# Half of the low parts of the MLP's second weight matrix: an accumulating DMA in place of a DVE subtraction

## The chip, the cores and the metric

One core of one Trainium2 chip. The metric is device microseconds of one execution of the whole program. The engines are named as the profile does: PE (TensorE, matmuls; PEld is its loading of weights), DVE (VectorE), ACT (ScalarE), POOL (GpSimd) and SP (SyncE, which here issues loads).

## The reference, cut to what matters

One decoder layer on 256 tokens of width 2048, all in float32: a normed input projection feeds sparse attention and retention, their gated sum is projected back, cross-attention and an MLP follow, and a final norm. The change touches the MLP's second product alone:

```python
def hybrid_layer(h, mem, ...):
    ...
    nm = rmsnorm(h, mlp_norm_w)
    h = h + jnp.square(jax.nn.relu(nm @ w_up)) @ w_down     # w_down: (8192, 2048), 64 MB
    return h

def reference(...):
    ...
    return rmsnorm(h, final_norm_w)
```

## The kernel before

Every weight passes through the core once, in chunks of 1 MB: 128 partitions by 2048 float32 values. A chunk's way is always the same. SP loads it from DRAM into a `raw` tile (three buffers). Then `chunk` cuts it into two halves of 1024 columns, and `split` makes two tiles of each half: ACT copies it to `hi`, rounded to the format that PE multiplies in one pass (float32r), and DVE subtracts, `lo = raw - hi`. `hi` and `lo` have four buffers each (`NHI`), so two chunks. The activations are split in the same way into a high and a low part. PE computes high times high, low times high and high times low, so three matmuls stand where one float32 product would be.

In `w_down` the activations are the stationary side (`xgroup`). For each row tile of 128 weights rows and each of the two token tiles, PE does `hi` with the activations' high part, `hi` with their low part, and `lo` with their high part, in that order, each over 512 columns: 12 matmuls per half, 24 per chunk. The product is done in two passes `f` over 4096 hidden channels, each after its own `w_up` stage; a pass has four column blocks `j` of 8 chunks. This makes 64 chunks. The first pass's `w_down` runs from about 1402 to 1559 us of the span, the second's from about 1765 to 1938 us.

In the last block (f = 1, j = 3) the last two chunks go through another branch of `xgroup` (`last`): both are loaded and split first, and then their matmuls run token tile by token tile. At the end of the first block of the second pass, `down_evac` takes one of the three `raw` buffers for the final norm's weights and keeps it to the end.

The work is written in the order of the main stream. A scheduler places each engine's instructions at build time, gives out the buffers and adds the waits: a buffer is given to a new tile when all readers of the old one are done, so the load of a new chunk waits for the last reader of an old `raw`, and the copy to a new `hi` for the last matmul with the old one. `pin` holds an order only in the program's first stage; here it does nothing.

POOL does a few small operations and DMAs in earlier stages. In the MLP it has nothing before the final norm's power.

Of the kernel before, what the change touches and what calls it, by code (L numbers as in the profile page):

```python
# [11 lines left out]
AF = mybir.ActivationFunctionType  # L12
ALU = mybir.AluOpType
# [4 lines left out]
P = 128  # L18
T = 256
D = 2048  # L20
EPS = 1e-6
# [44 lines left out]
class Kern:  # L66
# [15 lines left out]
        self.hung = 0  # L82
        self.ordered = False

    # ---- tiles
    def nm(self, s):
        self.n += 1
        return f"{s}_{self.n}"
# [22 lines left out]
    def pot(self, name):  # L111
        return self.po.tile([P, 512], F32, name=self.nm(name), tag="po")

    # ---- order: a step of the main stream is one tick; work hung on a later tick goes between steps
    def after(self, n, fn):
        self.hung += 1
        self.due.append((self.ticks + n, self.hung, fn))
# [11 lines left out]
        while self.due:  # L129
            self.tick()  # L130

    # streams in turns, each with its number of steps a turn
    def run(self, *gens):
        gens = [list(g) + [0.0] if isinstance(g, tuple) else [g, 1, 0.0] for g in gens]
        while gens:
            for item in list(gens):
                item[2] += item[1]
                while item[2] >= 1:
                    item[2] -= 1
                    try:  # L140
                        next(item[0])
                    except StopIteration:
                        gens.remove(item)
                        break
                    self.tick()
# [2 lines left out]
        for g in gens:  # L148
            yield from g

    # ---- arithmetic
    # while the pipeline fills, each engine keeps the order of the program
    def pin(self, ins):
        if self.ordered:
            self.tc.keep_in_program_order(ins)
# [1 line left out]
    def mul(self, out, l, r, start, stop):  # L157
        self.pin(self.nc.tensor.matmul(out, l, r, start=start, stop=stop, skip_group_check=True))  # L158

    # hi + lo == src, both exact in the tensor engine's one-pass format  # L160
    def split(self, hi, lo, src):
        self.pin(self.nc.scalar.activation(hi, src, AF.Copy))  # L162
        self.pin(self.nc.vector.tensor_tensor(lo, src, hi.bitcast(F32), op=ALU.subtract))  # L163

    # the same for src * scale, with a scale per partition
    def split_scaled(self, hi, lo, src, scale):
        self.pin(self.nc.scalar.activation(hi, src, AF.Copy, scale=scale))
        self.pin(self.nc.vector.scalar_tensor_tensor(lo, src, scale, hi.bitcast(F32), op0=ALU.mult, op1=ALU.subtract))

    # (v * s + EPS) ^ -0.5  # L170
    def rsqrt(self, out, v, s):
        self.nc.vector.tensor_scalar(out, v, s, EPS, op0=ALU.mult, op1=ALU.add)
        self.nc.gpsimd.tensor_tensor(out, out, self.mhalf.to_broadcast(out.shape), op=ALU.pow)
# [1 line left out]
    def bcast(self, R):  # L175
        return R[:, None, :].to_broadcast([P, 4, T])

    # tanh(y / 2) in place: sigmoid(y) = (1 + tanh(y / 2)) / 2
    def half_tanh(self, y):
        self.nc.scalar.activation(y, y, AF.Tanh, scale=0.5)  # L180

    # ---- the stream of weights
    def raw(self):
        return self.st.tile([P, 2048], F32, name=self.nm("raw"), tag="raw", bufs=3)

    # weights of kt row tiles, n columns; lists of hi and lo per row tile
    def chunk(self, src, kt, n, first=None):
        raw = self.raw()[:, :kt * n].rearrange("p (k n) -> p k n", k=kt)
        src = src.rearrange("(k p) n -> p k n", p=P)
        parts = 2 if first else 1  # L190
        for j in range(parts):
            if j:
                self.second()
            s = slice(j * kt // parts, (j + 1) * kt // parts)
            self.pin(self.nc.sync.dma_start(raw[:, s, :], src[:, s, :]))
        hs, ls = [], []
        m = 1024 // n
        for k in range(0, kt, m):
            h = self.st.tile([P, m, n], F32R, name=self.nm("hi"), tag="hi")
            l = self.st.tile([P, m, n], F32R, name=self.nm("lo"), tag="lo")  # L200
            self.split(h, l, raw[:, k:k + m, :])
            if first and k == 0:
                first()
            hs += [h[:, j, :] for j in range(m)]
            ls += [l[:, j, :] for j in range(m)]
        return hs, ls

    # out[col, t]: weights stationary
    def wgroup(self, w, c0, xh, xl, evac, rows=D):
        nkt = rows // P  # L210
        ps = self.mmt("w")
# [12 lines left out]
                evac(ps.rearrange("p (b t) -> p b t", b=4))  # L224
            yield

    # out[t, col]: activations stationary
    def xgroup(self, w, c0, xh, xl, evac, r0=0, rows=D, n=512, last=False, first=None):
        nkt = rows // P
        ps = [self.mmt("x")]  # L230
        ps = [self.mmt("x")[:, :n], ps[0][:, :n]] if last else [ps[0][:, 0:n], ps[0][:, 512:512 + n]]

        def part(kt, i, h, l):
            o = ps[i]
            s = slice(i * P, (i + 1) * P)
            a, c = xh[kt // 4][:, kt % 4, s], xl[kt // 4][:, kt % 4, s]
            self.mul(o, a, h, kt == 0, False)
            self.mul(o, c, h, False, False)
            self.mul(o, a, l, False, kt == nkt - 1)

        ck = 2048 // n
        end = nkt - 2 * ck if last else nkt
        for kt in range(end):
            k = kt % ck
            if k == 0:
                h, l = self.chunk(w[r0 + kt * P:r0 + (kt + ck) * P, c0:c0 + n], ck, n, first if kt == 0 else None)
            for i in range(2):
                part(kt, i, h[k], l[k])
            if kt == nkt - 1:
                for i in range(2):  # L250
                    evac(i, ps[i])
            yield
        if last:
            hs, ls = [], []
            for kt in range(end, nkt, ck):
                h, l = self.chunk(w[r0 + kt * P:r0 + (kt + ck) * P, c0:c0 + n], ck, n)
                hs += h
                ls += l
            for i in range(2):
                for kt in range(end, nkt):  # L260
                    part(kt, i, hs[kt - end], ls[kt - end])
                evac(i, ps[i])
                yield

    # four column tiles of src's two token tiles, transposed and split with the gain w
    def load_part(self, name, src, w, hs, ls, c, halves=False):
        x = self.big(name + "x", F32, (2, 512))

# [50 lines left out]

        return turn, split, spill, squares  # L320

    # 1 / rms per token, as a column and along each row
    def load_rms(self, s8, rs, R):
        nc = self.nc
        nc.vector.tensor_reduce(rs, s8, axis=AX.X, op=ALU.add)
# [59 lines left out]
    def retention(self):  # L385
        nc, a, rs = self.nc, self.a, self.rs
# [107 lines left out]

        self.ordered = True
        s8 = self.keep("xs8", [2, 4])
        # the tensor engine at its full clock by the time that the weights are there
        warm = self.pst("warm")

        def spin(n):  # L500
# [4 lines left out]
        turn, split, spill, squares = part(0)  # L505
# [8 lines left out]
        group = self.X(OFF["q_r"], rotary(qrT), first=rest)  # L514
        for c in range(4):
# [3 lines left out]
            if c < 3:  # L519
                turn, split, spill, squares = part(c + 1)  # L520
# [25 lines left out]
        self.flush()  # L546
        self.orh, self.orl = orh, orl

    # tanh of half the gate, tokens on the partitions
    def gate(self, dst):  # L550
        def evac(i, ps):
            if i == 0:
                dst.append(self.big("gate", F32, (2, 512)))
            self.nc.scalar.activation(dst[-1][:, i, :], ps, AF.Tanh, scale=self.hrs[:, i:i + 1])
        return evac
# [3 lines left out]
        self.nc.vector.tensor_tensor(o, ps, self.bcast(self.R), op=ALU.mult)  # L559
        self.kvc.append(o)  # L560

    # the overlapping windows of one of k, v with their position codes: [d, l, (g, c)], hi next to lo
    def blocks(self, which):
        nc = self.nc
        kT = self.kvc[which]
# [62 lines left out]
    def keys(self):  # L628
        nc, a, rs, R = self.nc, self.a, self.rs, self.R
        V, A, G, PE = nc.vector, nc.scalar, nc.gpsimd, nc.tensor  # L630
        self.mask = self.keep("mask", [800])
        self.tc.keep_in_program_order(nc.sync.dma_start(self.mask, a["c_mask"]))
        # columns of a group's keys: sel tile 1 | sel tile 0 | compressed | win tile 0 | win tile 1
        kcat = self.kcat = [self.big(f"kcat{g}", F32R, (2, 528)) for g in range(4)]
        self.vh, self.vl = {}, {}
        self.qh, self.ql = [], []
# [218 lines left out]
                          *[self.X(OFF["gate_a"] + 512 * j, self.gate(ga)) for j in range(4)]))  # L855
        self.flush()

    # h += f * ps; the split of h * w; the sum of squares
    def residual(self, dst, base, w, hs, ls, f, acc=None):
        nc = self.nc  # L860
        V, A = nc.vector, nc.scalar
# [22 lines left out]
    def merge(self):  # L884
        nc, a = self.nc, self.a
# [15 lines left out]
                        self.after(4 + 3 * n, lambda n=n: turn(j, n))  # L901
            return evac

        # the merged branches with channels on the partitions
        def turn(j, n):
            pt = self.pst("mT")
            for b in range(2):
# [117 lines left out]
    def mlp(self):  # L1025
        nc, a = self.nc, self.a
# [1 line left out]
        hres = [None] * 4  # L1028
        s8, r2 = self.keep("hs8", [2, 4]), self.keep("r2", [2])

        # the residual with tokens on the partitions, and its mean square
        def back(j, i):
            if i == 0:
                hres[j] = self.big("hres", F32, (2, 512))
# [24 lines left out]
        f8, ft = self.keep("fs", [2, 4]), self.keep("ft", [2])  # L1059
        fw, outs = [], []  # L1060

        # hidden = relu(u)^2 with u not yet divided by the rms: 1 / (mean square) at the end
        def down_evac(f, j):
            def evac(i, ps):
                o = hres[j][:, i, :]
# [29 lines left out]
        for f in range(2):  # L1095
            hh, hl = [], []
            self.run(self.seq(*[self.wgroup(a["w_up"][0], f * 4096 + 512 * j, self.h2h, self.h2l, up_evac(hh, hl))
                                for j in range(8)]))
            self.run(self.seq(*[self.xgroup(a["w_down"][0], 512 * j, hh, hl, down_evac(f, j), r0=f * 4096, rows=4096,
                                            last=(f == 1 and j == 3)) for j in range(4)]))  # L1100


def body(tc, a, out):
# [25 lines left out]
```

## Time and profile before

| | |
|---|---|
| Time, median of 2 runs | 1953.76 us (1953.6 to 1953.93) |
| Profiled execution, span from first to last instruction | 1951.9 us |
| Runs above that span | 1.9 us |
| PE / DVE / ACT / POOL busy, share of the span | 99% / 59% / 48% / 4% |
| Granted TensorE clock, mean | 0.999 |

The profiled execution has no time of its own beside its span; the 1.9 us are the difference to the median of the runs. A busy PE says that matmuls were in flight, not that they ran at the array's peak: a matmul's record is 0.40 us long here, and the next one starts before it ends. So the time of a stage is read from the starts.

### The profile page before, as it was taken

The page shows a single profiled execution, that of the slowest core. Times are in us where ns is not written, and L with a number is a line of the kernel's source. Part 1 is how long each engine was busy: PE and PEld are TensorE (multiplying, and loading weights), DVE is VectorE, ACT ScalarE, POOL GpSimd, SP SyncE. Part 2 cuts the span into 40 slices and gives each one's busy share as a digit, 9 for nine tenths or more (in the row PEclk, how much of TensorE's full clock was granted, in tenths as well). Part 3 has the DMA queues.
Part 4 walks back from the last instruction along what each step waited for, and adds up shares of the span by engine and source line. Part 5 has one row for each costly group of instructions (what it writes and reads, how often), then busy time and mean ns, then how long its engine had stood idle before and what let it go on. Part 6 is the DMA issues. An engine that isn't in the chain of part 4 may idle for free.

```text
span 1951.9 us, 28137 instructions
## 1 busy us (share of the span) xinstructions
PE 1933.5 (99%) x11606; PEld 1714.9 (88%) x11606; DVE 1145.7 (59%) x1327; ACT 937.3 (48%) x1214; POOL 85.3 (4%) x101
## 2 busy tenths in 40 slices
PE   8999999999999999999999999999999999999998
PEld 6888889888899999888889999999988899998886
DVE  6554577555756666886556756555544445554454
ACT  6444444454555555766445545544433344444442
POOL 1100021000000000321000000000000000000000
PEclk9999999999999999999999999999999999999999
DMA  7555544677876775434566654565655555655554
GB/s 269 210 174 192 186 172 175 229 249 245 274 248 244 248 254 176 137 112 140 184 208 232 208 173 154 172 191 177 193 184 184 193 189 179 189 178 194 188 179 151
DMA packets 190017, 382.29 MB, mean 196 GB/s; under 512 B 10576, under 2 KB 18768, under 8 KB 189760
## 3 DMA queue, kind: packets, MB, share of 16 engines
q1 hardware_dynamic: 185872, 375.01, 57.2%
q10 hardware_dynamic: 3216, 3.15, 0.5%
q0 software_dynamic: 800, 2.33, 0.4%
q8 instruction: 91, 1.49, 0.3%
q14 instruction: 38, 0.31, 0.0%
HBM read 374.17 MB, written 6.29 MB: 195 GB/s over the span
## 4 chain that ended last, share of the span: by engine, by line
PE 97%; DVE 1%; ACT 0%; issue 0%; DMA 0%; POOLq 0%; POOL 0%; DVEq 0%
PE x L158 52%; PE w L158 36%; PE acc L158 3%; PE o L158 1%; PE s L158 1%; PE ro L158 1%; PE pT L816 1%; DMA anw<-in_attn_norm_w_dram 0%; DVE lo L163 0%; PE tr L287 0%; PE rs L158 0%; ACT hi L162 0%; DVE bl L163 0%; PE xo L158 0%; PE g L158 0%
## 5 line engine op out<-in xcount | busy, mean ns | idle before, releaser
L163 DVE TENSOR_TENSOR lo<-raw,hi 128x1024 fp32r<-128x1024 f32 x688 | 848.6, 1240 | 702.8 <-ACT hi L162 688.1
L162 ACT ACTIVATE hi<-raw 128x1024 fp32r<-128x1024 f32 x688 | 724.1, 1059 | 913.2 <-PE x L158 526.0
L158 PE MATMUL w<-nh,hi 128*128 128x256 f32 x1088 | 308.2, 283 | 0.0
L158 PE MATMUL w<-nh,lo 128*128 128x256 f32 x1088 | 307.5, 283 | 0.0
L158 PE MATMUL w<-nl,hi 128*128 128x256 f32 x1088 | 306.9, 282 | 0.0
L158 PE MATMUL x<-hi,xh 128*128 128x512 f32 x704 | 282.5, 401 | 2.2 <-ACT hi L162 2.2
L158 PE MATMUL x<-hi,xl 128*128 128x512 f32 x704 | 278.0, 395 | 0.0
L158 PE MATMUL x<-lo,xh 128*128 128x512 f32 x704 | 277.2, 394 | 0.0
L158 PEld LDWEIGHTS w<-nl,hi 128*128 128x128 f32 x1088 | 207.1, 190 | 0.0
L158 PEld LDWEIGHTS w<-nh,hi 128*128 128x128 f32 x1088 | 207.1, 190 | 0.0
L158 PEld LDWEIGHTS w<-nh,lo 128*128 128x128 f32 x1088 | 206.8, 190 | 0.0
L158 PE MATMUL x<-hi,hl 128*128 128x512 f32 x512 | 202.7, 396 | 0.0
L158 PE MATMUL x<-hi,hh 128*128 128x512 f32 x512 | 202.3, 395 | 0.0
L158 PE MATMUL x<-lo,hh 128*128 128x512 f32 x512 | 201.0, 393 | 0.0
L158 PEld LDWEIGHTS x<-lo,xh 128*128 128x128 f32 x704 | 133.1, 189 | 30.9 <-DVE lo L163 0.8
L158 PEld LDWEIGHTS x<-hi,xh 128*128 128x128 f32 x704 | 132.8, 189 | 30.1 <-ACT hi L162 2.6
L158 PEld LDWEIGHTS x<-hi,xl 128*128 128x128 f32 x704 | 132.8, 189 | 26.5
L158 PE MATMUL w<-xh,hi 128*128 128x256 f32 x512 | 145.3, 284 | 0.0
L158 PE MATMUL w<-xh,lo 128*128 128x256 f32 x512 | 144.2, 282 | 0.0
L158 PE MATMUL w<-xl,hi 128*128 128x256 f32 x512 | 144.1, 281 | 0.0
L158 PEld LDWEIGHTS x<-lo,hh 128*128 128x128 f32 x512 | 96.6, 189 | 22.7
L158 PEld LDWEIGHTS x<-hi,hh 128*128 128x128 f32 x512 | 96.2, 188 | 23.1
(257 smaller groups left out, 2572.9 us busy)
## 6 DMA issues: line engine op xcount, KB each, us to landing
raw<-in_w_in_dram SPq DMA_DIRECT2D x119, 1024.0 KB, 4.9
raw<-in_w_up_dram SPq DMA_DIRECT2D x64, 1024.0 KB, 5.3
raw<-in_w_down_dram SPq DMA_DIRECT2D x64, 1024.0 KB, 5.1
raw<-in_cmp_w_k_dram SPq DMA_DIRECT2D x16, 1024.0 KB, 4.9
raw<-in_w_b_dram SPq DMA_DIRECT2D x16, 1024.0 KB, 5.2
raw<-in_cmp_w_v_dram SPq DMA_DIRECT2D x16, 1024.0 KB, 5.0
raw<-in_w_a_dram SPq DMA_DIRECT2D x16, 1024.0 KB, 5.1
raw<-in_w_out_dram SPq DMA_DIRECT2D x16, 1024.0 KB, 5.1
```

What stands on the lines that cost most here:

```text
L158: self.pin(self.nc.tensor.matmul(out, l, r, start=start, stop=stop, skip_group_check=True))
L162: self.pin(self.nc.scalar.activation(hi, src, AF.Copy))
L163: self.pin(self.nc.vector.tensor_tensor(lo, src, hi.bitcast(F32), op=ALU.subtract))
L816: PE.transpose(pt[:, r * P:(r + 1) * P], sms[r // 2][:, r % 2, c:c + P], self.ident)
```

## The change

`split_by_dma` takes the place of `split` for the second half of a chunk (`k` is 2) in the main loop of `w_down`; the first half keeps the subtraction. ACT writes `-round(raw)` into `lo`, GpSimd issues a DMA that adds `raw` onto `lo` in SBUF, and ACT copies `raw` to `hi`. `lo` is then `raw - round(raw)`, as before. The chunks of the `last` branch don't pass `adds` and stay as they were. The other lines of the diff take out comments.

```diff
+    def split_by_dma(self, hi, lo, src):
+        self.nc.scalar.activation(lo, src, AF.Copy, scale=-1.0)
+        self.nc.gpsimd.dma_start(lo, src, accum_op=ALU.add)
+        self.nc.scalar.activation(hi, src, AF.Copy)
...
-    def chunk(self, src, kt, n, first=None):
+    def chunk(self, src, kt, n, first=None, adds=False):
...
-            self.split(h, l, raw[:, k:k + m, :])
+            if adds and k:
+                self.split_by_dma(h, l, raw[:, k:k + m, :])
+            else:
+                self.split(h, l, raw[:, k:k + m, :])
...
-    def xgroup(self, w, c0, xh, xl, evac, r0=0, rows=D, n=512, last=False, first=None):
+    def xgroup(self, w, c0, xh, xl, evac, r0=0, rows=D, n=512, last=False, first=None, adds=False):
...
-                h, l = self.chunk(w[r0 + kt * P:r0 + (kt + ck) * P, c0:c0 + n], ck, n, first if kt == 0 else None)
+                h, l = self.chunk(w[r0 + kt * P:r0 + (kt + ck) * P, c0:c0 + n], ck, n, first if kt == 0 else None, adds)
...
-                                            last=(f == 1 and j == 3)) for j in range(4)]))
+                                            last=(f == 1 and j == 3), adds=True) for j in range(4)]))
```

## Rows read from the trace of the kernel before

**Rows 1.** The page: busy time by engine, and the chain by engine.
```profile
PE 1933.5 (99%) x11606; PEld 1714.9 (88%) x11606; DVE 1145.7 (59%) x1327; ACT 937.3 (48%) x1214; POOL 85.3 (4%) x101
...
PE 97%; DVE 1%; ACT 0%; issue 0%; DMA 0%; POOLq 0%; POOL 0%; DVEq 0%
```

**Rows 2.** Windows: busy us of PE, PEld, DVE, ACT, POOL, clock, DMA share, GB/s.
```profile
1402.50:1559.50 157.00, 157.00 (x678) 127.16 (x678) 74.80 (x64) 61.95 (x59) 0.00 (x0) 1.00 0.57 190
...
1810.00:1938.00 128.00, 128.00 (x552) 103.61 (x551) 62.50 (x62) 51.06 (x57) 0.00 (x0) 1.00 0.53 174
1938.00:1951.90 13.90, 5.46 (x24) 4.09 (x22) 5.67 (x12) 2.89 (x6) 1.10 (x2) 0.83 0.41 151
...
1934.50:1937.50 3.00, 3.00 (x15) 2.43 (x14) 0.00 (x0) 0.00 (x0) 0.00 (x0) 1.00 0.02 5
```

**Rows 3.** Timeline: matmul starts, and one half's copy and subtraction (start, length).
```profile
1403.41 0.40 PE L158 MATMUL x<-hi,hh 128*128 128x512 f32 x1
...
1406.44 0.40 PE L158 MATMUL x<-hi,hl 128*128 128x512 f32 x1
...
1419.44 1.06 ACT L162 ACTIVATE hi<-raw 128x1024 fp32r<-128x1024 f32 x1 [1.74 <-PE x L158]
...
1420.53 1.23 DVE L163 TENSOR_TENSOR lo<-raw,hi 128x1024 fp32r<-128x1024 f32 x1 [1.57 <-ACT hi L162]
...
1934.46 0.40 PE L158 MATMUL x<-hi,hl 128*128 128x512 f32 x1
...
1937.47 0.40 PE L158 MATMUL x<-lo,hh 128*128 128x512 f32 x1
```

**Rows 4.** Waits of POOL from 1390 to 1940 us: total us, times, longest.
```profile
POOL ft L1084 <- DVE ft L1083: 812.5, 1, 812.5
```

**Rows 5.** Lines from 1402.5 to 1559.5 us: busy us, mean ns, idle before.
```profile
L163 DVE TENSOR_TENSOR lo<-raw,hi 128x1024 fp32r<-128x1024 f32 x56 | 68.6, 1224 | 79.2 <-ACT hi L162 79.2
L162 ACT ACTIVATE hi<-raw 128x1024 fp32r<-128x1024 f32 x57 | 60.5, 1061 | 96.6 <-PE x L158 89.6 <-DVE lo L163 5.2 <-PE w L158 1.8
```

**Rows 6.** DMA of the first `w_down` stage: packets, MB, held share; us to landing.
```profile
q1 hardware_dynamic: 14962, 29.73, 56.7%
...
raw<-in_w_down_dram SPq DMA_DIRECT2D x28, 1024.0 KB, 5.1
```

**Rows 7.** Line 717, POOL's spill of `gate`: issue ns, us to landing.
```profile
L717 POOL DMA_DIRECT2D msp<-gate x4: 531/531/630, 482.9 to 562.6; - x4
...
DMA to landing us min/median/max: 3.2/3.3/3.5
```

**Rows 8.** DMA of 482 to 486 us and of 508 to 512 us.
```profile
q0 software_dynamic: 144, 0.52, 39.2%
...
raw<-in_w_b_dram SPq DMA_DIRECT2D x1, 1024.0 KB, 7.7
...
raw<-in_w_b_dram SPq DMA_DIRECT2D x1, 1024.0 KB, 5.3
```

**Rows 9.** SP's loads from 1775 us on (timelines), and waits from 1810 to 1935.
```profile
1789.35 0.34 SPq L1071 DMA_DIRECT2D raw<-in_final_norm_w_dram  x1
1794.90 128.77 SPq L195 DMA_DIRECT2D raw<-in_w_down_dram  x24
...
1822.85 0.37 SPq L195 DMA_DIRECT2D raw<-in_w_down_dram  x1
...
1839.55 0.37 SPq L195 DMA_DIRECT2D raw<-in_w_down_dram  x1
...
ACT hi L162 <- DMA raw<-in_w_down_dram: 7.8, 3, 2.8
...
SPq L195 <- DVE lo L163: 105.1, 21, 7.0
```

**Rows 10.** Windows of half a microsecond while one load runs (last: DMA share, GB/s).
```profile
1824.00:1824.50 0.50, 0.50 (x3) 0.38 (x2) 0.10 (x1) 0.37 (x1) 0.00 (x0) 1.00 0.80 82
...
1826.00:1826.50 0.50, 0.50 (x4) 0.41 (x3) 0.00 (x0) 0.40 (x1) 0.00 (x0) 1.00 1.04 406
```

## The prediction

> **What bounds the kernel now.** I read the page's busy line and its chain first: TensorE (PE) is busy for 99% of the span and makes up 97% of the chain that ended last [rows 1]. Then the stage of the change alone. The second multiplication of the MLP (`w_down`) runs twice, in the windows of [rows 2]: PE busy without a gap, DVE about 48%, ACT about 40%, the sixteen DMA engines 57% and 53%. Then the order inside the stage. A chunk is 512 rows of weights, split in two halves of 1024 columns, and each half feeds 12 matmuls that start 0.232 us apart [rows 3]. So a half lasts 2.79 us and a chunk 5.57 us, which is also the spacing of the loads, (1839.55 - 1822.85) / 3 [rows 9]. Last, the waits: ACT waits for PE to free a buffer, DVE waits for ACT, PE for nobody [rows 2, 5]. PE sets the pace; DVE, ACT and the loads follow it with time to spare.
>
> How much time: `hi` and `lo` have four buffers each, a buffer is free when PE has ended the half four back, and the new content is needed three halves later, 8.36 us. The copy to `hi` takes 1.06 us and the subtraction 1.23 us [rows 3, 5], so a half is ready about 6 us early.
>
> **The change, part by part.** The program has 64 chunks of `w_down`; the last two go through the `last` branch, which doesn't pass `adds`. So 62 odd halves change, one per chunk.
>
> *Removed:* 62 subtractions of 1.224 us [rows 5], 76 us of DVE. PE did not wait for DVE, so this gives 0. Could the matmuls run faster beside a quieter DVE? From 1934.5 to 1937.5 DVE and ACT are idle and the DMA engines nearly so [rows 2], and there 13 starts take (1937.47 - 1934.46) us, 0.232 us each; with all of them at work 13 take (1406.44 - 1403.41) us, 0.233 us each [rows 3]. So nothing is gained, and the bound below is 0.
>
> *Added on ACT:* 62 copies with scale -1, as long as the copy to `hi`, 1.06 us [rows 5]. ACT then does 3.2 us in a chunk of 5.57 us: hidden. The copy to `hi` of that half, now behind the negated copy in ACT's queue, is ready at about 2.2 us of its 8.36 us. If this cover were gone, each chunk would pay at most 1.06 us.
>
> *Added on GpSimd (POOL):* 62 DMA issues, 0.53 to 0.63 us each as in the spill of `gate` [rows 7]. POOL has nothing else to do from the last norm to the end, 812 us [rows 4], so nothing is queued behind a waiting issue: 0.
>
> *The wait that is added.* PE's third matmul of an odd half needs `lo`, and all later matmuls stand behind it. The negated copy ends 1.1 us after the buffer is free, so the DMA may take 8.36 + 0.46 - 1.1 = 7.7 us from issue to landing. No row shows a transfer from SBUF to SBUF or one that adds. The nearest are four POOL transfers of the same 512 KB from SBUF to DRAM: 3.2 to 3.5 us to landing [rows 7], in which the 16 engines were held for 39.2% of 4 us, 1.57 us [rows 8]. An addition reads two operands, `raw` and `lo`, and writes one. Lower bound: the second read costs nothing, 1.57 us held, 3.3 us to landing. Middle: the second read costs another pass, 3.14 us held, 4.9 us to landing. Upper: read, read and write follow one another, 4.7 us held, 6.5 us to landing. I take the middle, since it counts the bytes that must be read, and keep both ends. Even the upper end is under 7.7 us while the transfer is alone, so what decides is that it isn't alone.
>
> The weight loads hold the engines for 56.7% of the stage [rows 6], 0.567 x 5.57 = 3.16 us a chunk. Beside the first spill a 1 MB load took 7.7 us to land, beside the second 5.3 us, against 5.1 us in this stage [rows 6, 8]: the two queues can cost each other time, so I add up their held times. The Trainium skill says why ("DMA: Bandwidth & Descriptors", section "Issuing engines are not separate DMA queues"): DMAs from any issuing engine run on the same 16 DMA engines and interleave. By that rule the sum is the one below; by separate queues the change would cost nothing before the two-buffer stretch below. The 7.7 us row agrees, without proving it.
>
> Adding: 3.16 + 3.14 = 6.30 us of DMA engines in a chunk that PE does in 5.57 us. The DMA engines would then set the pace: 0.73 us x 62 = 45 us. With the lower end, 4.73 us, they don't; with the upper end, 7.87 us, it is 2.30 x 62 = 143 us.
>
> *The raw buffers.* The transfer also holds `raw` until it has landed, and the next load into that buffer, on SP's queue, waits for it (as it does for DVE now [rows 9]); behind it in SP's queue stand only later loads. For 40 chunks there are three raw buffers: the loop of load 5.1, copy 1.06, negated copy 1.06, transfer 4.9 and about 0.2 of wake-ups is 12.3 us of the 16.7 us that three chunks give. From the load of the final norm's weights at 1789 us on, one of the three is taken, and 24 loads go through two [rows 9]. There the loop has 11.14 us: a transfer above 3.7 us makes it the bound. It is already the one place where ACT waits for a load (7.8 us, three times) [rows 9]. With 4.9 us alone it asks for 6.2 us a chunk, under the 6.30 us above; if loads and additions fully stretch each other, 5.1 + 1.6 and 4.9 + 1.6, it is 7.7 us, and 22 chunks would pay 32 us more than counted. Against that stands that a load holds the engines while it hardly moves anything: in a half microsecond near its start 82 GB/s at a share of 0.80, later 406 GB/s [rows 10]. Packets of the other queue might move there. These two have opposite signs and similar size; I take neither.
>
> **Sum.** Removed 0, ACT 0, POOL 0, DMA engines +45 us on the profiled execution's 1951.9 us; the runs lie 1.9 us above the span, for work around it that the change doesn't touch. 1953.8 + 45 = 1999 us.
>
> **The rivals.**
>
> *Hidden.* The second read runs beside the write: 4.73 us held of 5.57. Only the two-buffer stretch could feel it: 3.3 us alone is under 3.7 us, stretched by up to 1.5 us it costs half of that less 0.4 over 22 chunks, at most 12 us. 1954 to 1966 us. For it: DMA share 57% and a short spill. Against it: two operands of 512 KB have to be read.
>
> *Bytes, not held time.* At the full rate of about 400 GB/s [rows 10] a load needs 2.6 us and two reads 2.6 us: 5.2 us, under 5.57, if the slow start of each transfer is filled by the other queue. Then only the two-buffer stretch pays: (12.3 - 11.14) / 2 = 0.58 us x 22 = 13 us, up to 30 us with some stretching: 1967 to 1985 us. The Trainium skill speaks for this one ("Collectives: The Full Stack", section "The bandwidth ceiling: the fold count and why AG ≠ RS ≠ AR"): an adding transfer is slower because it reads two sources, and the addition costs nothing. No row here shows it.
>
> *The addition is slower than its reads.* If a row's write waits for both of its reads, 4.7 us are held and PE runs at the DMA engines' 7.87 us a chunk in all 62: 2097 us, and more if the engines sit idle between the rows of one transfer. It decides from about 2.4 us held per addition, where 3.16 and the addition exceed 5.57. For it: the operation is one that no row shows, on every engine at once. Against it: nothing in the trace.
>
> *Faster.* It would need PE to run closer than 0.232 us, or a wait on DVE that PE doesn't have [rows 2].
>
> **How the numbers follow.** A measurement of this kernel can tell about 2%, 39 us, from no change. Forecast, 1985 to 2040 us: 0.34, of which 0.04 lies below 1993 us. Hidden: 0.17. Bytes: 0.22. Slower addition, 2040 us and above: 0.25. Faster: 0.02. So faster by over 2%: 0.02; within 2%: 0.17 + 0.22 + 0.04 = 0.43; slower: 0.30 + 0.25 = 0.55. The range goes from the hidden case, 1955 us, to the upper bound of the addition, 2100 us; beyond lie about half of the slowest case, 0.12, and some 0.06 below. The forecast's own range is 1985 to 2040 us.
>
> **What the changed profile would show.** DVE's `lo<-raw,hi` down by 62, ACT's copies up by 62, POOL with 62 issues. The software queue with 62 transfers of 512 KB, at some 28% (one pass), 50% (two) or more of the stage. The matmul with `lo` in the chain waiting for a POOL DMA, PE idle by 0.7 us a chunk, chunks 6.3 us apart, the DMA share near 1. If the bytes rival is right, three-buffer chunks stay at 5.57 us and the later ones spread. If the addition is slow, its landing takes over 7.7 us and the spacing is the same in both stretches. What would make the forecast wrong most of all is the held time of one addition, for which the nearest row is a plain transfer; then ACT's order, if the negated copy were put behind later copies; and the granted clock, which is 1.00 while PE is never idle and 0.83 in the last window, where it is [rows 2]: waits inside the stage might cost more than their length.

## The result, and the profile after

| | |
|---|---|
| Time, median of 2 runs | 2058.43 us (2055.69 to 2061.18) |
| Before | 1953.76 us |
| Ratio | 1.0536, 95% interval 1.0518 to 1.0553 |
| Profiled execution, span | 2053.9 us, before 1951.9 us |
| Granted TensorE clock, mean | 0.984, before 0.999 |

The change costs 105 us, 5.4%. The forecast was 45 us, so the direction was right and the size less than half. The page first, its busy line, its chain by engine and by line:

```profile
PE 1969.1 (96%) x11606; PEld 1729.7 (84%) x11606; DVE 1070.8 (52%) x1265; ACT 992.7 (48%) x1276; POOL 138.7 (7%) x163
...
PE 79%; DMA 15%; issue 3%; ACT 2%; DVE 1%; POOL 0%; POOLq 0%; SPq 0%; ACTq 0%; DVEq 0%
PE x L158 36%; PE w L158 35%; DMA lo<-raw 11%; DMA raw<-in_w_down_dram 3%; PE acc L158 3%; PE o L158 1%; ACT lo L167 1%; PE s L158 1%; ACT hi L169 1%; PE ro L158 1%; PE pT L825 0%; DVE lo L163 0%; DMA anw<-in_attn_norm_w_dram 0%; PE tr L296 0%; DMA rep<-in_c_rep_dram 0%
```

Against [rows 1]: DVE lost 75 us, ACT gained 55, POOL 53, and PE's share of the chain fell from 97% to 79%. What took its place is the adding DMA (`lo<-raw`, 11%) and the loads (3%), which were not in the chain before. PE's own busy time grew by 36 us for the same matmuls.

Next, where it happened. POOL issues one addition per chunk, so the spacing of its issues is the spacing of the chunks. The timeline of POOL, the first and last issue of the first pass (32 issues), and of a part of the second pass with one raw buffer gone (19 issues):

```profile
1399.62 0.92 POOL L168 DMA_DIRECT2D lo<-raw  x1 [271.83 <-ACT lo L167]
...
1595.14 0.86 POOL L168 DMA_DIRECT2D lo<-raw  x1 [6.54 <-ACT lo L167]
...
1863.55 0.86 POOL L168 DMA_DIRECT2D lo<-raw  x1 [5.17 <-ACT lo L167]
...
2023.80 0.86 POOL L168 DMA_DIRECT2D lo<-raw  x1 [8.01 <-ACT lo L167]
```

With three raw buffers a chunk takes (1595.14 - 1399.62) / 31 = 6.31 us, with two (2023.80 - 1863.55) / 18 = 8.90 us; before it was 5.57 us throughout. So 40 chunks lose 0.73 us each, 29 us, and 22 chunks lose 3.3 us each, 73 us: 102 us, the difference of the two spans. Most of the loss lies in the smaller part.

The two stretches have different bounds. The windows, PE's busy time first, the last three columns the granted clock, the DMA engines' share and GB/s:

```profile
1402.50:1590.00 187.50, 171.80 (x716) 135.05 (x714) 42.92 (x39) 93.42 (x92) 25.77 (x30) 0.98 0.92 246
...
1840.00:2040.00 200.00, 154.52 (x553) 116.36 (x552) 37.56 (x41) 70.04 (x80) 18.94 (x22) 0.88 0.68 174
```

And the DMA queues from 1402.5 to 1595.5 and from 1862 to 2024 us, q1 with the loads and q0 with the additions: packets, MB, share of the engines' time.

```profile
q1 hardware_dynamic: 15910, 31.60, 48.1%
q0 software_dynamic: 4387, 15.94, 44.3%
...
q1 hardware_dynamic: 9504, 18.88, 39.4%
q0 software_dynamic: 2593, 9.44, 29.4%
```

With three buffers the engines are held 92% of the time (before: 57% [rows 2, 6]), near a bound. With two they are held 68%: here they have time, and the chunks are still slower. What is late there is read from the chain between 1907 and 1925 us, one turn of one raw buffer (start, length, what):

```profile
1907.22 6.23 DMA raw<-in_w_down_dram
...
1914.52 1.04 ACT hi L169
1915.56 0.96 ACT lo L167
1916.52 0.28 issue
1916.80 8.13 DMA lo<-raw
...
1925.06 6.15 DMA raw<-in_w_down_dram
```

The load lands, ACT copies the first half to `hi` (0.96 us, from 1913.56), the second half to `hi` (1.04), negates (0.96), POOL starts 0.28 us later, the addition lands after 8.13 us, and only then does SP load into the buffer again: 1925.06 - 1907.22 = 17.84 us for two chunks, with PE nowhere in it. The waits from 1862 to 2024 us say the same, in total us, times and longest; the last is SP's:

```profile
ACT hi L162 <- DMA raw<-in_w_down_dram: 92.7, 17, 6.8
PEld x L158 <- DMA lo<-raw: 48.3, 19, 4.3
...
SPq L201 <- DMA lo<-raw: 159.4, 19, 9.0
```

One thing was not as the diff is written. ACT's timeline shows the copy to `hi` (line 169) ahead of the negated copy (line 167), in all 62 chunks; the scheduler had turned them round:

```profile
1408.63 1.06 ACT L169 ACTIVATE hi<-raw 128x1024 fp32r<-128x1024 f32 x1 [0.74 <-PE x L158]
1409.60 1.04 ACT L167 ACTIVATE lo<-raw 128x1024 fp32r<-128x1024 f32 x1
```

### The profile page after: what moved, and what is told of

Its sections match the earlier page's. It is cut to its first block, busy times and chain, and to the rows that moved or that the text cites. A ratio compares the mean times of both kernels' runs of the same rounds, so it can differ in the third digit from the quotient of the medians.

```text
span 2053.9 us, 28340 instructions
## 1 busy us (share of the span) xinstructions
PE 1969.1 (96%) x11606; PEld 1729.7 (84%) x11606; DVE 1070.8 (52%) x1265; ACT 992.7 (48%) x1276; POOL 138.7 (7%) x163
## 4 chain that ended last, share of the span: by engine, by line
PE 79%; DMA 15%; issue 3%; ACT 2%; DVE 1%; POOL 0%; POOLq 0%; SPq 0%; ACTq 0%; DVEq 0%
PE x L158 36%; PE w L158 35%; DMA lo<-raw 11%; DMA raw<-in_w_down_dram 3%; PE acc L158 3%; PE o L158 1%; ACT lo L167 1%; PE s L158 1%; ACT hi L169 1%; PE ro L158 1%; PE pT L825 0%; DVE lo L163 0%; DMA anw<-in_attn_norm_w_dram 0%; PE tr L296 0%; DMA rep<-in_c_rep_dram 0%
## 5 line engine op out<-in xcount | busy, mean ns | idle before, releaser
L163 DVE TENSOR_TENSOR lo<-raw,hi 128x1024 fp32r<-128x1024 f32 x626 | 773.1, 1242 | 871.3 <-ACT hi L162 848.8
L162 ACT ACTIVATE hi<-raw 128x1024 fp32r<-128x1024 f32 x626 | 658.0, 1058 | 886.1 <-PE x L158 358.6
L158 PE MATMUL x<-lo,hh 128*128 128x512 f32 x512 | 215.7, 423 | 65.5 <-DMA lo<-raw 65.4
L158 PE MATMUL x<-hi,hh 128*128 128x512 f32 x512 | 211.9, 414 | 0.5 <-ACT hi L162 0.4
L158 PE MATMUL x<-hi,hl 128*128 128x512 f32 x512 | 210.9, 412 | 0.0
L158 PEld LDWEIGHTS x<-lo,hh 128*128 128x128 f32 x512 | 102.1, 200 | 105.6 <-DMA lo<-raw 82.4
L158 PEld LDWEIGHTS x<-hi,hh 128*128 128x128 f32 x512 | 102.6, 200 | 24.7 <-ACT hi L162 1.1
```

## The experiments

Theory 1: two losses. With three raw buffers the DMA engines' time is the bound; with two, the loop of load, copies, addition and next load. Theory 2, the rival: each addition costs the same wherever it stands, because it is slow or lands too late for PE. Further rivals: ACT's order, the issue and the wait as such, and loads slowed by the traffic alone.

**What one transfer costs (`alone`).** A kernel of DMAs only: six of each kind in turn, each addition or copy waiting for the one before. In the parts with loads at most two loads are in flight.

```python
for _ in range(6):
    nc.gpsimd.dma_start(lo, src, accum_op=ALU.add)     # line 91; then copies, line 94
...
for _ in range(6):
    nc.gpsimd.dma_start(lo.bitcast(F32), src, accum_op=ALU.add)     # line 97
...
for _ in range(10):
    load()                                             # line 79: 1 MB from SP
for _ in range(6):
    nc.gpsimd.dma_start(lo, src, accum_op=ALU.add)     # line 105; then copies, line 110
```

> No part of the layer is computed: this kernel does only six additions of 512 KB (SBUF onto a float32r tile) one after the other, six plain copies of the same tile, six additions onto float32, six loads of 1 MB alone, then additions beside a stream of loads (two in flight) and copies beside the same stream. If an addition costs two passes, it holds the engines for about 3.1 us against 1.6 of a copy and lands 1.5 us later (4.9 against 3.3). If the addition itself is slow, it takes over 6 us even alone. If it is the sharing that makes it slow, it takes 4 to 5 us alone and 7 to 9 us beside the loads, and the loads land later beside additions than beside copies.

The queue rows of the windows from 7 to 36 us (additions alone) and 36.5 to 56 us (copies alone), then the landings, counted from the issue: additions, copies, additions onto float32, loads alone (with the first two of the next group), then additions beside loads and those loads, copies beside loads and those loads.

```profile
q0 software_dynamic: 864, 3.15, 57.2%
...
q0 software_dynamic: 864, 3.15, 44.5%
...
DMA to landing us min/median/max: 4.5/4.5/4.6
...
DMA to landing us min/median/max: 2.9/2.9/2.9
...
DMA to landing us min/median/max: 4.5/4.5/4.5
...
DMA to landing us min/median/max: 5.1/5.4/7.7
...
DMA to landing us min/median/max: 4.5/7.3/9.3
DMA to landing us min/median/max: 6.1/7.7/9.6
...
DMA to landing us min/median/max: 4.4/6.8/7.9
DMA to landing us min/median/max: 6.7/8.1/9.6
```

An addition holds the engines for 0.572 x 29 / 6 = 2.76 us and lands after 4.5 us, a copy 0.445 x 19.5 / 6 = 1.45 us and 2.9 us. So the addition costs 1.9 copies, and it is not slow alone. Beside a stream of loads, with the engines held 95% of the time or more, it lands after 7.3 us; but a copy takes 6.8 us there too. It is the sharing that makes it late. One part of the expectation did not come: the loads landed no later beside additions (7.7 us) than beside copies (8.1 us). The Trainium skill ("Collectives: The Full Stack", section "The bandwidth ceiling: the fold count and why AG ≠ RS ≠ AR") says that ReduceScatter, whose add needs two source reads, gets half the bandwidth of AllGather, which copies, with a measured ratio of 1.93. That is a collective over four ranks; the ratio of the held times here, inside one core, is 1.91 and agrees. The prediction took this as speaking for the rival "bytes", but two reads are what its middle term counts as well, so it doesn't choose between the two.

**Three raw buffers throughout (`own_buffer`).** The norm's weights go into the large pool:

```diff
-                    fw.append(self.raw())
-                    nc.sync.dma_start(fw[0], a["final_norm_w"].partition_broadcast(P))
+                    for n in range(2):
+                        fw.append(self.big("fn"))
+                        nc.sync.dma_start(fw[n] ..., a["final_norm_w"][n * 1024:(n + 1) * 1024].partition_broadcast(P))
...
```

> The changed kernel, but the final norm's weights go into two tiles of the large pool, so that all 62 additions run with three raw buffers. Theory 1, the loop through two raw buffers (load, copies, addition, next load) costs 3.3 us a chunk and makes some 73 of the 102 us: 62 x 0.73 = 45 us over the kernel before, 1999 us (1990 to 2010). Theory 2, each addition costs the same wherever it stands: no change, 2050 to 2060 us.

Measured 2002.44 us, ratio 1.0252 (1.0235 to 1.0269): 48 us over before, where theory 1 had 45, and 56 us of the loss gone by moving 8 KB per partition. Theory 2 falls. POOL's first and 32nd issue:

```profile
1399.75 0.92 POOL L168 DMA_DIRECT2D lo<-raw  x1 [271.83 <-ACT lo L167]
...
1597.35 0.86 POOL L168 DMA_DIRECT2D lo<-raw  x1 [4.61 <-ACT lo L167]
```

6.37 us a chunk, now in both passes. The control, the same edit to the kernel before (`before_own_buffer`):

> Control: the kernel before with the final norm's weights in the large pool. PE waits for no load there, so no change by either theory: 1952 to 1956 us.

Measured 1953.44 us, ratio 0.9998 (0.9989 to 1.0008). The buffer matters only with the additions.

**The two stretches apart.** Additions in the first pass alone (`first_pass_only`, `adds=(f == 0)`):

> The changed kernel with additions in the first pass over w_down alone, 32 of them, all with three raw buffers, ACT's order as in the changed kernel. If the parts add up: 32 x 0.73 = 23 us, 1977 us (1974 to 1981). If what is lost here is made good later, less.

Measured 1977.16 us, ratio 1.0115 (1.0099 to 1.0132): 23 us, as expected. And in the last three column blocks alone (`two_buffers_only`, `adds=(f == 1 and j > 0)`):

> The changed kernel with additions in the last three column blocks of the second pass alone, 22 of them, all while the norm's weights hold one raw buffer. If the loop through two raw buffers costs 3.3 us a chunk: 22 x 3.3 = 73 us, 2022 to 2030 us. If each addition costs the same: 22/62 of 104 us, 37 us, 1991 us.

Measured 2022.35 us, ratio 1.0350 (1.0335 to 1.0366): 68 us for 22 additions, 3.1 us each, where the 32 of the first pass cost 0.7 us each. With the 8 chunks that neither has, 6 us by the same price, the parts make 98 of the 105 us. The chain of this kernel, load and addition of one buffer:

```profile
1909.00 6.25 DMA raw<-in_w_down_dram
...
1918.60 8.01 DMA lo<-raw
```

The load of one buffer and the addition of the other start within a microsecond of each other (in the changed kernel 1907.22, and 1907.98 for the addition before), so each pair runs side by side, turn after turn.

**ACT's order (`negated_first`, `own_negated_first`).** The order as written, held by the scheduler's own means:

```diff
-        self.nc.scalar.activation(lo, src, AF.Copy, scale=-1.0)
+        self.tc.keep_in_program_order(self.nc.scalar.activation(lo, src, AF.Copy, scale=-1.0))
         self.nc.gpsimd.dma_start(lo, src, accum_op=ALU.add)
-        self.nc.scalar.activation(hi, src, AF.Copy)
+        self.tc.keep_in_program_order(self.nc.scalar.activation(hi, src, AF.Copy))
```

> The changed kernel with ACT held to the written order, the negated copy ahead of the copy to hi of the same half (in the changed kernel it came out behind it). Theory 1: 0.96 us of the 17.8 us loop falls away where there are two raw buffers, 0.48 us x 20 = 10 us, 2048 us; nothing with three. If ACT's order were the main cost, 0.96 us would fall away in every chunk, 60 us, about 2000 us. If the DMA engines are the bound everywhere, no change, 2058 us.

Measured 2036.36 us, ratio 1.0417 (1.0378 to 1.0455), with runs from 2025 to 2045 us: 22 us better, twice what theory 1 expected and a third of what the order would give if it were the main cost. With three raw buffers as well:

> As own_buffer, with the negated copy ahead of the copy to hi on ACT. Theory 1, engine time: each addition starts 1 us earlier, but the engines have no more time: 1998 to 2004 us. Rival, the length of one chain from a free lo to the landing (now 1.06 + 0.96 + 0.3 + 5.7 of 8.8 us, with 9.2 us landings too late): 1 us more slack takes away much of the loss, 1960 to 1980 us.

Measured 1989.24 us, ratio 1.0182 (1.0165 to 1.0199): 13 us better than own_buffer, where theory 1 had expected nothing and its rival 20 to 40 us. So neither was right: engine time is not the whole of the 0.8 us a chunk. POOL's first and 32nd issue, and a window of the first pass, in this kernel and then in own_buffer:

```profile
1398.24 0.92 POOL L168 DMA_DIRECT2D lo<-raw  x1 [271.01 <-ACT lo L167]
...
1586.09 0.86 POOL L168 DMA_DIRECT2D lo<-raw  x1 [6.24 <-ACT lo L167]
...
1402.50:1559.50 157.00, 146.84 (x623) 116.14 (x623) 38.45 (x34) 81.37 (x80) 22.33 (x26) 1.00 0.96 255
...
1402.50:1559.50 157.00, 145.16 (x593) 114.53 (x592) 35.93 (x33) 77.03 (x76) 20.62 (x24) 0.96 0.91 241
```

6.06 us a chunk and a DMA share of 0.96. A load's 3.16 us [rows 6] and an addition's 2.76 us make 5.92 us, so this kernel is nearly at the floor of engine time. own_buffer stood 0.3 us above it, at 6.37 us and a share of 0.91, and the order is what was changed. How the order costs that isn't parted further: the granted clock differs with it, 0.96 against 1.00.

**Less engine time (`own_every_other`, `own_first_copy`, `plain_copy`).** Every second chunk only, with three raw buffers, by a flag in front of `split_by_dma`:

```diff
-            if adds and k:
+            if adds and k and self.turns():
```

> As own_buffer, but only every second chunk has its odd half's low part made by the DMA: 31 additions. Theory 1, the DMA engines' time is the bound with three raw buffers: a pair of chunks needs 2 x 3.16 + 2.76 = 9.1 us of the 11.15 us that PE takes, so nothing is lost: 1954 to 1960 us. Rival, each addition lands too late for PE by itself: half of own_buffer's 48 us, 1978 us.

Measured 1955.21 us, ratio 1.0009 (0.9999 to 1.0018), and PE without a gap in the first pass:

```profile
1402.50:1559.50 157.00, 157.00 (x678) 127.14 (x678) 57.68 (x50) 75.25 (x73) 12.02 (x14) 1.00 0.80 235
```

31 additions, in the worse order, cost nothing: the addition, its issue and the wait for it are no loss by themselves where the engines have time (share 0.80). This doesn't part engine time from late landing, since they landed earlier too, in the first pass after 4.6 us in the middle and 5.6 us in own_buffer. In the same direction, a copy in place of the addition (`self.nc.gpsimd.dma_start(lo, src)`), with three buffers and the negated copy first:

> Three raw buffers, the negated copy first, and a plain copy in place of the addition (the low parts of these halves are wrong, and so is the output): 3.16 + 1.45 = 4.6 us of DMA engines in a chunk. If engine time is what own_negated_first still pays for: back to 1954 to 1958 us. If the wait for a transfer costs by itself, 10 to 20 us stay.

Measured 1955.98 us, ratio 1.0011 (1.0002 to 1.0020). As many issues, waits and buffers, with 4.6 instead of 5.9 us of engine time, leave 2 us of own_negated_first's 35. Its copies landed after up to 8.1 us in the first pass, and PE waited there for one of them, 1.1 us. And the copy in the changed kernel, with its two-buffer stretch and its order:

> The changed kernel with the DMA copying raw into lo without adding (the low parts of these halves are then wrong, and the output with them): the same issues, waits and buffers, without the second read. Theory 1: the engines are held for 3.16 + 1.6 = 4.8 us a chunk, so three-buffer chunks go back to 5.57 us; the loop through two buffers shrinks from 17.8 to about 14.5 us, 1.7 us a chunk x 20 = 34 us: 1985 to 1995 us. If the issue by POOL and the wait itself cost the time, not the addition, it stays near 2050 us.

Measured 1988.40 us, ratio 1.0174 (1.0154 to 1.0195), inside the expected range, but not by its terms: between POOL's issues a chunk takes 5.79 us in the first pass, where 5.57 was expected, and 6.90 us with two buffers, where 7.25 was. The loop through two buffers costs even with copies.

**Traffic without waits (`before_side_additions`).** The kernel before, with one addition per chunk between two tiles of their own:

```diff
             self.split(h, l, raw[:, k:k + m, :])
+            if adds and k:
+                self.nc.gpsimd.dma_start(self.side[1], self.side[0], accum_op=ALU.add)
...
```

> The kernel before (all low parts by DVE, the norm's weights in the large pool) plus 64 additions of 512 KB from POOL between two tiles that nothing else reads, one after the other, beside the same loads. They take engine time but nobody waits for them and no raw is held. If the loss comes through the waits (for lo, and for raw), 1954 to 1960 us. If loads slowed by the additions alone starve PE, 1975 to 2000 us.

Measured 1990.20 us, ratio 1.0179 (1.0148 to 1.0210): by the time alone this looks like the rival, and it isn't. (62 additions were issued; the last two chunks have none.) The window of the first pass, and the end of the chain:

```profile
1402.50:1559.50 157.00, 157.00 (x679) 127.26 (x678) 76.53 (x66) 62.02 (x59) 19.82 (x23) 1.00 0.97 264
...
1975.23 0.86 POOL side L203
1976.09 0.59 POOL ft L1089
```

With the engines held 97% of the time PE lost nothing, 679 matmuls against 678 [rows 2]. The additions fell behind, 23 where PE did 28 chunks, and the last of them kept POOL from the final norm's power (`ft`) until 1976 us. The 36 us are nearly all that queue, an effect of this experiment. What it shows is that loads with enough buffers bear the sharing; an addition that must keep up with PE doesn't. It also shows the bound without any wait of PE: from the first of these additions, 1411.6 us, to 1559.5 us the engines' share is 1.00, and in these 148 us there was room for 23 additions, 6.4 us for each, beside loads at PE's 5.57 us.

**More low buffers (`own_more_lo`).** The tile of every second addition in the large pool:

> As own_buffer, with the low tile of every second adding half in the large pool: in effect six lo buffers in place of four. Theory 1, engine time: the mean of 3.16 + 2.76 = 5.92 us a chunk stays above 5.57 us, so at least 0.35 x 62 = 21 us stay, 1976 to 1995 us. Rival, single late landings with engine time to spare: more buffers hide them, 1955 to 1965 us.

Measured 2034.50 us, ratio 1.0415 (1.0399 to 1.0430): slower, and neither theory's range. The scheduler put the additions in pairs, as POOL's timeline shows:

```profile
1436.98 0.85 POOL L168 DMA_DIRECT2D lo<-raw  x1 [11.73 <-ACT lo L167]
1438.88 0.85 POOL L168 DMA_DIRECT2D lo<-raw  x1 [1.04 <-ACT lo L167]
1451.53 1.81 POOL L168 DMA_DIRECT2D lo<-raw  x2 [11.80 <-ACT lo L167]
```

With two additions at once and then none for 12 us it tests another order, not more buffers. It decides nothing.

No version beats the kernel before: the best, with every second chunk, is equal to it, since PE was busy for 99% of the time to begin with.

## Why the prediction was wrong

- **PE bounds, DVE's 76 us give nothing:** right. DVE fell by 75 us and no version is faster than before.
- **An addition costs two passes, 3.14 us held, 4.9 us to landing:** right in kind, 2.76 us and 4.5 us alone. Two copies of 1.45 us make 2.9 us; the transfer taken from [rows 8], 1.57 us and to DRAM, was a little dear.
- **Engine times add up, 6.30 us a chunk:** the changed kernel shows 6.31 us with three buffers, but that the numbers meet is luck. Engine time accounts for about 5.9 to 6.06 us, and ACT's order for the other 0.3 us (own_negated_first); the 0.38 us too much for the addition stood in for the order, which was put at nothing. That engine time is a bound at all is shown by the two kernels with less of it, both without loss, and by before_side_additions, whose engines were full at 6.4 us for each addition.
- **The two-buffer stretch, where I took neither correction: the step that failed.** It was counted at 6.30 us a chunk like the rest, with 7.7 us as its upper end; it is 8.90 us. 22 chunks x 2.6 us = 57 us, nearly all of the 60 us that were missing. own_buffer, which takes the stretch away, comes out at 2002 us, where the forecast for the whole was 1999. The forecast had the engines full and still priced this loop with each transfer alone, 12.3 us for two chunks; the chain shows 17.84 us. The addition lands after 8.1 us, not 4.9 (6.5 at the upper end), since it runs beside a load at every turn; the load takes 6.2 us, not 5.1 (6.7); the copy to `hi` of the second half, which I had placed behind the negated copy, is inside the loop with 1.0 us; and the wake-ups make 0.5 us, 0.28 of them POOL's start, where 0.2 was allowed. I also let a gain from the loads' slow start stand against the stretching, and no row had shown such a gain.
- **ACT's order:** ACT's added copy was put at nothing, with the negated copy first, and another order was named as something that could make the forecast wrong. Another order came, and cost 13 us with three buffers throughout and 22 us in the changed kernel.
- **The rivals:** "hidden" and "bytes" both needed the engines to have time, and with three buffers the engines were held 0.92 to 0.96 of it. "Slower addition" gave nearly the measured time, for a cause that isn't there: 2.76 us held, not 4.7, and a spacing that differs between the stretches.

## What to carry to other kernels

A DMA that takes over an engine's work also takes over that engine's place among the readers of a buffer: follow the buffer's whole turn, from load to next load, at the fewest buffers that any stretch has, with each transfer priced beside the other one and not alone. An adding transfer in SBUF counted as two copies of engine time here, and added to the loads it must stay below the time of a chunk. And the written order of two independent instructions on an engine need not be the order on the chip, as in these 62 chunks: read it from the timeline.

## What the runs showed of the hardware that was not expected

POOL takes 0.85 us to issue an addition of 512 KB and 0.53 us for a copy; whether the addition goes onto float32r or float32 makes no difference (4.5 us both). And TensorE's clock fell during the waits of the two-buffer stretch. The changed kernel's half microseconds, PE's busy time first and the clock third from the right:

```profile
1912.50:1913.00 0.50, 0.26 (x2) 0.00 (x0) 0.00 (x0) 0.00 (x0) 0.00 (x0) 1.00 0.97 213
...
1915.00:1915.50 0.50, 0.00 (x0) 0.00 (x0) 0.50 (x1) 0.50 (x2) 0.00 (x0) 0.50 0.09 16
```

PE had been without a matmul since the first of them when the clock went from 1.00 (2.4 GHz) to 0.50 (1.2 GHz). In that stretch it cost nothing that the chain shows, since PE isn't in it; whether it adds to the 6.3 us with three buffers, where the mean was 0.98 (0.96 in own_buffer and 1.00 in own_negated_first), wasn't tried.
